# A hybrid decoder layer on one core: the FFN's planned order without lag between TensorE's steps, with leads by kind of step, and with the sums of weights and of activations in tiles of their own

## The chip, the cores and the metric

One Trainium2 chip, one of its cores. The metric is the time of one execution on the device in microseconds (us); lower is better.

## The reference, cut to what matters

The layer is a mixer (state-space and RWKV heads) followed by a gated FFN with a causal convolution. The change lies in the FFN:

```python
D_MODEL, SEQ, D_FF, FFN_CONV = 1024, 2048, 2816, 3
hn = _rms_norm(h, pre_ffn_norm)
u = _causal_dwconv(hn @ ffn_w_up, ffn_conv_w, ffn_conv_b)      # 2 * D_FF columns, 3 taps
gate, val = jnp.split(u, 2, axis=-1)
f = (jax.nn.silu(gate) * val) @ ffn_w_down
h = h + _rms_norm(f, post_ffn_norm)
```

Everything is float32. The kernel multiplies in float16: each operand is split into a high and a low half, and a product is three matmuls (high by high, high by low, low by high).

## The kernel before, in words

`phase_R` (RWKV) and `phase_S` (SSD, output projection, first norm) come first; then `phase_F`, the FFN. `phase_F` takes the tokens in two halves of 1024. For each of 22 blocks of hidden columns, counted by f, `Up.run` computes a gate and a value block with seven products in place of eight (a Strassen-like scheme in 2 by 2 blocks). Each product is 12 matmuls of 128x128 by 128x512 on line 1378, so an f has 84. Its weights are seven tiles `w0` to `w6`, one buffer each. In the first half they are made on the spot, in `Up.weights`: four blocks of `w_u` are loaded to a ring of six tiles `us`; POOL (GpSimd) forms sums of them, one into a small tile `ut` and the others in place in `us` (line 1350); ACT (ScalarE) writes the high half of `w` (line 1219) and DVE (VectorE) the low half (line 1226); SP (SyncE) stores each `w` in DRAM (line 1347). In the second half they are only loaded from there.

After the products of an f: ACT and DVE gather the PSUM banks into `C0` (one buffer) and `C1` (two buffers), on lines 1392 and 1396. ACT scales (line 1427), DVE adds two taps for the gate block `p` and two for the value block `a` (line 1431), ACT applies silu (line 1441), and DVE multiplies (line 1444). POOL copies the two carried columns in and out (`fcarry`, lines 1435 and 1437).

Two f make a pair. `Pair.factors` splits the pair's result into seven tiles `fa`: DVE sums in place (`p`, line 1484), POOL sums into a small tile `ft` (line 1484, two writes to the same tile), ACT writes the high halves (line 1219), POOL the low halves (line 1224). `down` then multiplies two pairs (at the end of a half, three) by the down weights: 168 matmuls on line 1614. Its weights `dw` are made from `r` (loads of 1 MB), with POOL sums in `r` and `rt` (line 1193), high halves on ACT (line 1575), low halves on DVE (line 1578), four tiles in a ring. DVE adds the banks to accumulators `acc` (line 1627). In the last down of the first half one pair has its weights in `dwx`, which borrows `C0`, `C1` and `a1`. `Half.tokens` loads and splits the activations into `b0` to `b6`, with a POOL sum in a small tile `ht`. `Finish.rows` does the last norm: squares into a scratch tile `fj` (line 1690), gains (line 1693), and the output rows `fin` (line 1706).

The small tiles `ht`, `ut`, `ft` and `fj` share one ring of two buffers with the tag `s3`. Each step that begins a use of it also "writes" the name `"s3"`, so that the uses follow each other in the order of the program text:

```python
op("G", 1.25, lambda: sub(x(), st[a11], st[a21]), (n[a11], n[a21]), (nt, "s3"))              # ut
(o, "s3") if o == nt and not t else (o,)                                                      # ft, both writes
```

What sets the order: `phase_F` doesn't emit its steps from f = 2 on, it hands them to a planner, `Program` (`op` is `Program.add`). A step has an engine (T for TensorE or PE, V for DVE, A for ACT, G for POOL, Q for SP's queue), an estimated duration, a function, and the names that it reads and writes. `Program.run` fixes TensorE's order as the text has it, gives each step a due time (counted back from the TensorE step that needs it), and then simulates the five engines: whenever one is free, the step with the earliest due time among the ready ones starts; an engine with a ready step never waits. A step's result is there after the step's duration and a lag of its engine, `LAG`. The simulated order is the order in which each engine's queue is written, and the engines then run their queues strictly in that order. In the text, the order is: steps of f, weights of f + 1, then every fourth f the down of two earlier pairs, then, at odd f, the factors of the pair. `last_down`, the down of the last pairs of the second half with the final norm, is emitted outside the planner, as is everything before f = 2.

Of the kernel before, what the change touches and what calls it, by code (L numbers as in the profile page):

```python
# [7 lines left out]
F32 = mybir.dt.float32  # L8
# [8 lines left out]
T = 2048  # L17
# [38 lines left out]
class Program:  # L56
# [2 lines left out]

    SHARED = 0.55, 0.75  # L60
    STORE = 4.0
    LAG = {"T": 0.25, "V": 0.12, "A": 0.14, "G": 0.12, "Q": 2.0}

    def __init__(self):
        self.on, self.ops, self.writer, self.readers, self.tensor, self.near, self.far = False, [], {}, {}, None, set(), set()

    def add(self, engine, us, fn, reads=(), writes=()):
        if not self.on:
            fn()
            return  # L70
        n = len(self.ops)
        before = set()
        for r in reads:
            if r in self.writer:
                before.add(self.writer[r])
            self.readers.setdefault(r, []).append(n)
        for w in writes:
            if w in self.writer:
                before.add(self.writer[w])
            before.update(self.readers.pop(w, ()))  # L80
            self.writer[w] = n
        if engine == "T":
            if self.tensor is not None:
                before.add(self.tensor)
            self.tensor = n
        if engine == "V" and any(r[0] in ("u", "d") for r in reads):
            self.near.add(n)
        if engine == "Q" and not writes:
            self.far.add(n)
        before.discard(n)  # L90
        self.ops.append((engine, us, fn, before))

    def run(self):
        ops = self.ops
        count = len(ops)
        after = [[] for _ in ops]
        for n, (_, _, _, before) in enumerate(ops):
            for b in before:
                after[b].append(n)
        due, at = [1e9] * count, 0.0  # L100
        for n, (engine, us, _, _) in enumerate(ops):
            if engine == "T":
                due[n] = at
                at += us
        for n in range(count - 1, -1, -1):
            engine, us, _, _ = ops[n]
            for a in after[n]:
                due[n] = min(due[n], due[a] - us - self.LAG[engine])
        left = [len(o[3]) for o in ops]
        ready = [0.0] * count  # L110
        wait = {k: [] for k in self.LAG}
        for n in range(count):
            if not left[n]:
                wait[ops[n][0]].append(n)

        now, order, busy, coming = 0.0, [], {}, []
        while len(order) < count or busy:
            for k, some in wait.items():
                if k in busy:
                    continue  # L120
                some = [n for n in some if ready[n] <= now + 1e-9]
                if some:
                    n = min(some, key=lambda n: (due[n], n))
                    wait[k].remove(n)
                    order.append(n)
                    busy[k] = [ops[n][1], n]
            rate = dict.fromkeys(busy, 1.0)
            if "V" in busy and "G" in busy and busy["V"][1] not in self.near:
                rate["V"], rate["G"] = self.SHARED
            step = min([v[0] / rate[k] for k, v in busy.items()] + [  # L130
                ready[n] - now for k, some in wait.items() if k not in busy for n in some])
            now += step
            for k in list(busy):
                busy[k][0] -= step * rate[k]
                if busy[k][0] < 1e-9:
                    n = busy.pop(k)[1]
                    for a in after[n]:
                        ready[a] = max(ready[a], now + self.LAG[k] + self.STORE * (a in self.far))
                        left[a] -= 1
                        if not left[a]:  # L140
                            wait[ops[a][0]].append(a)
        for n in order:
            ops[n][2]()
        self.__init__()
# [32 lines left out]
S_RIGHT = (  # L177
    "ident_s mhalf_s", "ssm pov por ss pnv pnr", "Y", "yr", "xi", "m", "gpost", "gpre2", "hT", "yt", "wo",
)
F_EARLY = ("us", "s3", "b0", "b1", "b2", "b3")  # L180
F_MID = (
    "p0", "p1", *(f"w{i}" for i in range(7)), "C0", "b4", "b5", "b6", "C1", "a1", "fpar mhalf_f fcarry",
)
# [979 lines left out]
def phase_F(tc, K, w_u, w_d, H, HN, out, halves=2):  # L1163
# [6 lines left out]
    with ExitStack() as ctx:  # L1170
# [25 lines left out]
            S.activation(hi, src, AF.Copy)  # L1196
            eng.tensor_tensor(out=lo, in0=src, in1=hi, op=ALU.subtract)

        def temp(name):
            return wk.tile([P, Q], F32, name=name, tag="s3", bufs=2)  # L1200

        prog = Program()
        op = prog.add
# [27 lines left out]
        class Half:  # L1231
# [10 lines left out]
            def part(self, k, wanted, nm):  # L1242
# [20 lines left out]

                        op("Q", 1., load, (), (name, "us" if ring else ("p", q)))
                n11, n21, n12, n22 = names
                nt = slot("s3", 2)

                def hold(*some):
                    return (*some, *(x[:2] for x in some if x[0] == "p"))
# [14 lines left out]

                def x():
                    if "t" not in h:
                        h["t"] = temp(f"ht{nm}{k}")
                    return h["t"]

                put(0, n11, lambda: h[0, 0])  # L1290
                minus(n12, n12, n11, lambda: (h[1, 0], h[1, 0], h[0, 0]))
                op("G", 1.25, lambda: sub(x(), h[1, 1], h[1, 0]), hold(n22, n12), (nt, "s3"))
                put(1, nt, x)
                put(2, n12, lambda: h[1, 0])
                if 3 in wanted:
# [8 lines left out]
        class Up:  # L1304
# [6 lines left out]
            def weights(self):  # L1311
# [11 lines left out]
                for s, c in ((1, 0), (0, 0), (1, 1), (0, 1)):  # L1323
# [6 lines left out]
                            pace(tc, K, d, 12)  # L1330

                    op("Q", .9, load, (), (n[s, c], "us"))
                nt = slot("s3", 2)

                def x():
                    if "t" not in st:
                        st["t"] = temp("ut" + nm).rearrange("p (a b) -> p a b", b=P)
                    return st["t"]

                def put(i, name, get):  # L1340
# [10 lines left out]

                a11, a12, a21, a22 = (0, 0), (0, 1), (1, 0), (1, 1)
                put(0, n[a11], lambda: st[a11])
                op("G", 1.25, lambda: sub(x(), st[a11], st[a21]), (n[a11], n[a21]), (nt, "s3"))
                plus(a21, a21, a22, ALU.add)
                plus(a11, a21, a11)
                put(1, n[a11], lambda: st[a11])
# [91 lines left out]
        class Pair:  # L1449
# [8 lines left out]
            def factors(self, u0, u1):  # L1458
                nm, a = self.nm, self.a
                tag = "w{}" if self.extra else f"fa{{}}{self.i % 2}"  # L1460
                nt, t = slot("s3", 2), []
                n11, n21, n12, n22 = ("p", 0, 0), ("p", 0, 1), ("p", 1, 0), ("p", 1, 1)
                src = {n11: (u0, 0), n21: (u0, Q), n12: (u1, 0), n22: (u1, Q)}

                def get(n):
                    if n == nt:
                        if not t:
                            t.append(temp("ft" + nm))
                        return t[0]
                    u, x = src[n]  # L1470
                    return u.p[:, x:x + Q]

                def put(i, n):
                    def parts():
                        if i not in a:
                            a[i] = wk.tile([P, 2, Q], F16, name=f"fa{i}{nm}", tag=tag.format(i))
                        return get(n), a[i][:, 0, :], a[i][:, 1, :]

                    hold = (n[:2],) if n != nt else ()
                    split_op((*self.fa[i], 0), (*self.fa[i], 1), parts, "V" if self.extra else "G", (n, *hold), ())  # L1480

                def plus(o, x, y, alu, e="G"):
                    hold = [n[:2] for n in (x, y) if n != nt]
                    op(e, {"G": 1.25, "V": .62}[e], lambda: {"G": G_, "V": V}[e].tensor_tensor(
                        out=get(o), in0=get(x), in1=get(y), op=alu), (x, y, *hold), (o, "s3") if o == nt and not t else (o,))

                put(0, n11)
                plus(nt, n11, n21, ALU.subtract)
                put(3, nt)
                plus(n21, n21, n22, ALU.add, "V")  # L1490
                plus(n11, n21, n11, ALU.subtract, "V")
                put(1, n11)
                plus(nt, n12, n11, ALU.subtract)
                put(4, n12)
                put(2, n21)
                put(5, nt)
                put(6, n22)
# [153 lines left out]
        class Finish:  # L1651
# [14 lines left out]
            def rows(self, q, t, eng, folded=False):  # L1666
# [10 lines left out]

                op("Q", 2., load, (), (nx,))
                for first, dh in zip((True, False), (1, 0) if q else (0, 1)):
                    nj = slot("s3", 2)  # L1680
                    nacc = ("acc", y[dh], t)

                    def c(dh=dh):
# [2 lines left out]
                    def square(c=c, dh=dh, first=first):  # L1686
                        if first:
                            x["ss"] = wk.tile([P, 2], F32, name=f"fss{tt}", tag="fss", bufs=2)
                        jk = wk.tile([P, 2 * Q], BF16, name=f"fj{tt}{dh}", tag="s3", bufs=2)
                        S.activation(jk[:, 0:Q], c(), AF.Square, scale=IWS, accum_out=x["ss"][:, dh:dh + 1])  # L1690

                    def gain(c=c, dh=dh):
# [1 line left out]

                    if (q or dh) and not folded:
                        op("G", 1.25, lambda c=c: add(c(), c(), acc[1][:, t]), (nacc, ("acc", 1, t)), (nacc,))
                    op("A", .75, square, (nacc,), (nj, "s3", (*ns, dh), *(((*ns, 1 - dh), (*ns, "r")) if first else ())))
                    op("V" if eng is V else "G", .62 if eng is V else 1.25, gain, (nacc, "gf"), (nacc,))

                def sums():  # L1700
# [205 lines left out]
```

## Time and profile before

| what | value |
|---|---|
| median of 3 runs | 2689.52 us (2687.17 to 2689.76) |
| profiled execution, its own time | 2683.97 us |
| its span, first to last instruction | 2681.7 us |
| mean granted TensorE clock | 0.971 |
| PE busy | 2475.0 us, 92% of the span |
| DVE, ACT, POOL busy | 1909.1, 1207.9, 1223.6 us |
| the planned part, about | 1437 to 2614 us after the span's start |

The span is shorter than the execution's time by what lies around the instructions, and the profiled execution is 5.55 us below the median of the runs. Matmuls are pipelined, so PE busy near 100% is not PE at its peak; how many matmuls a stretch holds says more. "A <-B" behind an idle time names the instruction that ended it. A group's mean duration mixes undisturbed and delayed instructions.

### The profile page before, as it was taken

The numbers are of one execution on the slowest core, as the hardware profiler recorded it, in microseconds if no ns is written. First come the engines' busy times: TensorE is split into PE (matmuls) and PEld (weight loads), VectorE is DVE, ScalarE is ACT, GpSimd is POOL, SyncE is SP. The second block draws the span as 40 slices with busy tenths as digits, with TensorE's granted clock in tenths as the row PEclk, the third lists the DMA queues.
The fourth block names the chain that finished last, engine by engine and source line by source line (L and its number), as shares of the span: only waits on it lengthen the run. The fifth ranks groups of instructions, "written<-read, shape, count | busy, mean of one in ns | idle before, by whom it ended". The sixth has DMA issues, their size and how long they took to land. (4 is left out here: it accounts for less than half of the span.)

```text
span 2681.7 us, 53948 instructions
## 1 busy us (share of the span) xinstructions
PE 2475.0 (92%) x21340; PEld 1556.0 (58%) x21340; DVE 1909.1 (71%) x3655; ACT 1207.9 (45%) x2467; POOL 1223.6 (46%) x1324
## 2 busy tenths in 40 slices
PE   5889999999999889999997899999999999999998
PEld 4788888888888855555543344444443444444443
DVE  6768777777777665567677868787789836465557
ACT  6445555555565453344444543434354333123132
POOL 2344444444545343234467565656657523222135
PEclk8899999999999989999999999999999999999999
DMA  6323232232223252334455434443435543333252
GB/s 212 73 61 73 53 60 57 65 81 53 57 60 73 89 174 98 107 115 143 128 194 171 156 138 157 134 169 122 159 124 188 183 149 100 103 102 102 87 158 106
DMA packets 309341, 310.74 MB, mean 116 GB/s; under 512 B 168160, under 2 KB 213600, under 8 KB 305760
## 3 DMA queue, kind: packets, MB, share of 16 engines
q1 hardware_dynamic: 307792, 305.72, 37.9%
q8 instruction: 167, 2.74, 0.4%
q10 hardware_dynamic: 1296, 1.58, 0.2%
q14 instruction: 86, 0.70, 0.1%
HBM read 187.85 MB, written 110.99 MB: 111 GB/s over the span
## 5 line engine op out<-in xcount | busy, mean ns | idle before, releaser
L1378 PE MATMUL u<-b,w 128*128 128x512 f16 x3696 | 816.6, 383 | 30.4 <-ACT w L1219 16.1
L1378 PEld LDWEIGHTS <-w 128*128 128x128 f16 x3696 | 363.3, 99 | 480.0 <-issue 29.7
L289 PE MATMUL d<-xt,wr 128*128 128x129 f16 x5376 | 336.9, 224 | 18.1 <-DMA xt<-xh 15.3
L1614 PE MATMUL d<-dw,fa 128*128 128x512 f16 x1512 | 336.4, 381 | 10.6 <-DVE dw L1578 8.4
L289 PEld LDWEIGHTS <-wr 128*128 128x128 f16 x5376 | 322.8, 100 | 32.5 <-ACT wr L252 15.2
L1614 PEld LDWEIGHTS <-fa 128*128 128x128 f16 x1596 | 157.2, 98 | 212.9 <-issue 26.9
L1396 DVE TENSOR_TENSOR C<-u,C 128x512 f32<-128x512 f32 x220 | 150.5, 685 | 163.0 <-PE u L1378 162.6
L289 PE MATMUL c<-xt,wc 128*128 128x131 f16 x3072 | 205.3, 227 | 23.3 <-ACT tr L429 10.4
L289 PEld LDWEIGHTS <-wc 128*128 128x128 f16 x3072 | 189.4, 100 | 39.9 <-issue 31.9
L1627 DVE TENSOR_TENSOR acc<-d,acc 128x512 f32<-128x512 f32 x212 | 140.2, 682 | 51.8 <-PE d L1614 51.2
L576 DVE TENSOR_TENSOR tmp<-atl,xl 128x60 f32<-128x60 f32 (+24 forms) x465 | 139.5, 300 | 44.9 <-DMA atl<-ATd 28.7
L1431 DVE SCALAR_TENSOR_TENSOR p<-C,fpar,p 128x1024 f32<-128x1024 f32 x88 | 126.4, 1437 | 57.0 <-ACT p L1427 53.6
L1224 POOL TENSOR_TENSOR fa<-p,fa 128x512 f16<-128x512 f32 x100 | 133.2, 1350 | 70.8 <-ACT fa L1219 70.8
L1226 DVE SCALAR_TENSOR_TENSOR w<-us,w 128x512 f16<-128x512 f32 x132 | 116.5, 889 | 61.2 <-ACT w L1219 60.2
L452 DVE SCALAR_TENSOR_TENSOR ca<-rc,cw,ca 128x128 f32<-128x128 f32 x384 | 132.3, 389 | 22.8 <-POOL ca L447 22.6
L1219 ACT ACTIVATE fa<-p 128x512 f16<-128x512 f32 x110 | 66.5, 626 | 162.6 <-DVE p L1444 138.8
L579 DVE TENSOR_TENSOR xl<-xl,tmp 128x60 f32<-128x60 f32 (+24 forms) x465 | 124.7, 268 | 11.3
L1437 POOL COPY fcarry<-C 128x2 f32<-128x2 f32 x88 | 36.1, 410 | 182.6 <-DVE C L1396 182.2
L1431 DVE SCALAR_TENSOR_TENSOR a<-C,fpar,a 128x1024 f32<-128x1024 f32 x88 | 114.3, 1299 | 6.4 <-ACT a L1427 4.6
L1219 ACT ACTIVATE w<-us 128x512 f16<-128x512 f32 x132 | 80.0, 622 | 81.0 <-POOL us L1350 61.9
L1392 ACT ACTIVATE C<-u 128x512 f32<-128x512 f32 x88 | 51.8, 589 | 142.7 <-PE u L1378 125.7
L689 POOL TENSOR_TENSOR tS<-S,Pi 64x256 f32<-64x256 f32 x64 | 40.4, 632 | 163.5 <-DVE S L699 161.1
(316 smaller groups left out, 4550.3 us busy)
## 6 DMA issues: line engine op xcount, KB each, us to landing
UW<-w SPq DMA_DIRECT2D x154, 256.0 KB
w<-UW SPq DMA_DIRECT2D x154, 256.0 KB
us<-in_w_u_dram SPq DMA_DIRECT2D x88, 256.0 KB
DW<-dw SPq DMA_DIRECT2D x70, 256.0 KB
dw<-DW SPq DMA_DIRECT2D x56, 256.0 KB
hs<-HN SPq DMA_DIRECT2D x48, 256.0 KB
r<-in_w_d_dram SPq DMA_DIRECT2D x10, 1024.0 KB
xin<-in_x_dram SPq DMA_DIRECT2D x16, 512.0 KB
```

The source lines that it names most:

```text
L289: nc.tensor.matmul(ps, w[:, a, kt, :], xt[:, b, kt, cols], start=n == 0, stop=n == 3 * KT - 1)
L452: V.scalar_tensor_tensor(out=acc[:, q], in0=raw[:, q, k:k + 128], scalar=cw[:, g + q, k:k + 1], in1=acc[:, q], op0=ALU.mult, op1=ALU.add)
L576: chain.tensor_tensor(out=tmp[:, :m, :n], in0=atl[:, j, j + 1:32].unsqueeze(1).to_broadcast([P, m, n]), in1=xl[:, :m, j:j + 1].to_broadcas ...
L579: chain.tensor_tensor(out=xl[:, :m, j + 1:32], in0=xl[:, :m, j + 1:32], in1=tmp[:, :m, :n], op=ALU.add)
L1219: S.activation(h, src, AF.Copy, **({} if scale is None else {"scale": scale}))
L1224: {"V": V, "G": G_}[engine].tensor_tensor(out=l, in0=src, in1=h, op=ALU.subtract)
L1226: V.scalar_tensor_tensor(out=l, in0=src, scalar=scale, in1=h, op0=ALU.mult, op1=ALU.subtract)
L1378: nc.tensor.matmul(bk[at], self.w[i][:, u, k, :], self.half.b[i][:, k, v, :], start=start and n == 0, stop=n == 11, skip_group_check=True)
L1396: op("V", .61, lambda: V.tensor_tensor(out=part(j, x), in0=bk[at], in1=part(*a), op=ALU.add), (("u", 4 * s + at), (*(c0, c1)[a[0]], a[1])) ...
L1431: V.scalar_tensor_tensor(out=o[j], in0=C[j][:, 2 - d:1026 - d], scalar=cw[:, g, 2 - d:3 - d], in1=o[j], op0=ALU.mult, op1=ALU.add)
L1614: nc.tensor.matmul(bk[s, t], pairs[m].a[i][:, u, t * P:t * P + P], pairs[m].w[n][0][:, v, :], start=new and m == 0 and u == v == 0, stop=m ...
L1627: V.tensor_tensor(out=acc[j][:, t], in0=bk[s, t], in1=acc[j][:, t], op=ALU.add)
```

## The change

Four things, all in the planner's input or in the tiles; no arithmetic changes and no instruction is added or removed.

- Between two TensorE steps the planner no longer counts `LAG["T"]` (0.25), neither in the due times nor in the simulation.
- Each step gets a kind: its engine, the least of the names that it writes, the least of those it reads ("-" for none). `LEAD` maps 21 kinds to a number of microseconds. The choice among ready steps is by due time less lead.
- The ring `s3` of two becomes two tiles of one buffer each, `s3` and `s4`, with the same bytes in all: `ut` in `s3`, `ft` in `s4`, `ht` in `s4` for the first half and in `s3` for the second, the scratch `fj` in one or the other by its half of the columns.
- The name `"s3"` is no longer written, so uses of one tile follow each other only through that tile.

```diff
+    LEAD = {"A C0 u": 21, "A p p": 20, "A w us": 23, "G cy C1": 36, "G fa fa": 6, "G rt r": -38, "Q r -": -4, "Q us -": -40, "V C0 C0": 27, "V C1 C0": 9, "V C1 C1": 1, "V a1 C1": 7, "V acc acc": -4, "V b b": 3, "V dw dw": 2, "V hx acc": 11, "V p C0": 8, "V p a1": -2, "V p p": 7, "V w p": 16, "V w us": -4}
...
+        self.kinds.append(" ".join([engine, *(min([x[0] for x in some if isinstance(x, tuple)] or ["-"]) for some in (writes, reads))]))
...
             for a in after[n]:
-                due[n] = min(due[n], due[a] - us - self.LAG[engine])
+                if engine != "T" or ops[a][0] != "T":
+                    due[n] = min(due[n], due[a] - us - self.LAG[engine])
...
-                    n = min(some, key=lambda n: (due[n], n))
+                    n = min(some, key=lambda n: (due[n] - self.LEAD.get(self.kinds[n], 0.0), n))
...
-                        ready[a] = max(ready[a], now + self.LAG[k] + self.STORE * (a in self.far))
+                        lag = self.STORE * (a in self.far) + self.LAG[k] * (k != "T" or ops[a][0] != "T")
+                        ready[a] = max(ready[a], now + lag)
...
-F_EARLY = ("us", "s3", "b0", "b1", "b2", "b3")
+F_EARLY = ("us", "s3", "s4", "b0", "b1", "b2", "b3")
...
-        def temp(name):
-            return wk.tile([P, Q], F32, name=name, tag="s3", bufs=2)
+        def temp(name, tag):
+            return wk.tile([P, Q], F32, name=name, tag=tag)
...
-                op("G", 1.25, lambda: sub(x(), st[a11], st[a21]), (n[a11], n[a21]), (nt, "s3"))
+                op("G", 1.25, lambda: sub(x(), st[a11], st[a21]), (n[a11], n[a21]), (nt,))
...
-                nt, t = slot("s3", 2), []
+                nt, t = ("s4", 0), []
...
-                        out=get(o), in0=get(x), in1=get(y), op=alu), (x, y, *hold), (o, "s3") if o == nt and not t else (o,))
+                        out=get(o), in0=get(x), in1=get(y), op=alu), (x, y, *hold), (o,))
```

Kinds that the text below names: "A w us" and "V w us" are the high and low halves of the up weights, "Q us -" the loads of `us`, "A C0 u" and "V C1 C0" gathers of an up bank, "V p C0" and "V a1 C1" the taps, "A p p" silu, "V acc acc" the gathers of a down bank and the final gains, "V dw dw" and "V C0 C0" the low halves of `dw` and `dwx`, "G fa fa" the low halves of `fa`, "G rt r" sums into `rt`, "V hx acc" the output rows.

More of the change, by code (lines that the diff above doesn't have):

```diff
@@ L65, in __init__ @@
         self.on, self.ops, self.writer, self.readers, self.tensor, self.near, self.far = False, [], {}, {}, None, set(), set()
+        self.kinds = []
     def add(self, engine, us, fn, reads=(), writes=()):
@@ L1265, in part @@
                 n11, n21, n12, n22 = names
-                nt = slot("s3", 2)
+                nt = (f"s{4 - hf}", 0)
                 def hold(*some):
@@ L1286, in x @@
                     if "t" not in h:
-                        h["t"] = temp(f"ht{nm}{k}")
+                        h["t"] = temp(f"ht{nm}{k}", f"s{4 - hf}")
                     return h["t"]
@@ L1291, in part @@
                 minus(n12, n12, n11, lambda: (h[1, 0], h[1, 0], h[0, 0]))
-                op("G", 1.25, lambda: sub(x(), h[1, 1], h[1, 0]), hold(n22, n12), (nt, "s3"))
+                op("G", 1.25, lambda: sub(x(), h[1, 1], h[1, 0]), hold(n22, n12), (nt,))
                 put(1, nt, x)
@@ L1332, in weights @@
                     op("Q", .9, load, (), (n[s, c], "us"))
-                nt = slot("s3", 2)
+                nt = ("s3", 0)
                 def x():
                     if "t" not in st:
-                        st["t"] = temp("ut" + nm).rearrange("p (a b) -> p a b", b=P)
+                        st["t"] = temp("ut" + nm, "s3").rearrange("p (a b) -> p a b", b=P)
                     return st["t"]
@@ L1467, in get @@
                         if not t:
-                            t.append(temp("ft" + nm))
+                            t.append(temp("ft" + nm, "s4"))
                         return t[0]
@@ L1679, in rows @@
                 for first, dh in zip((True, False), (1, 0) if q else (0, 1)):
-                    nj = slot("s3", 2)
+                    nj = (f"s{3 + dh}", 0)
                     nacc = ("acc", y[dh], t)
@@ L1688, in square @@
                             x["ss"] = wk.tile([P, 2], F32, name=f"fss{tt}", tag="fss", bufs=2)
-                        jk = wk.tile([P, 2 * Q], BF16, name=f"fj{tt}{dh}", tag="s3", bufs=2)
+                        jk = wk.tile([P, 2 * Q], BF16, name=f"fj{tt}{dh}", tag=f"s{3 + dh}")
                         S.activation(jk[:, 0:Q], c(), AF.Square, scale=IWS, accum_out=x["ss"][:, dh:dh + 1])
@@ L1696, in rows @@
                         op("G", 1.25, lambda c=c: add(c(), c(), acc[1][:, t]), (nacc, ("acc", 1, t)), (nacc,))
-                    op("A", .75, square, (nacc,), (nj, "s3", (*ns, dh), *(((*ns, 1 - dh), (*ns, "r")) if first else ())))
+                    op("A", .75, square, (nacc,), (nj, (*ns, dh), *(((*ns, 1 - dh), (*ns, "r")) if first else ())))
                     op("V" if eng is V else "G", .62 if eng is V else 1.25, gain, (nacc, "gf"), (nacc,))
```

## The prediction

> **What bounds the kernel now.** I read, in this order, the page's totals and slices, the chain of waits, the table of three stretches, PE's waits, and then the order of each engine around one stall. A row of the chain gives PE's own pace:
>
> ```profile
> span 2681.7 us, 53948 instructions
> 2197.64 72.52 PE u L1378 x336
> ```
>
> 336 matmuls in 72.52 us without a stop are 0.2158 us each. Three stretches of the planned part (columns: window, its length, then busy time and count of PE, PE's loads, DVE, ACT and POOL, granted clock, DMA share, GB/s):
>
> ```profile
> 1437.00:2000.00 563.00, 527.29 (x2359) 232.07 (x2358) 445.61 (x515) 254.09 (x390) 340.02 (x285) 0.97 0.43 147
> 2000.00:2082.00 82.00, 70.62 (x311) 30.80 (x309) 81.60 (x90) 33.58 (x64) 57.42 (x43) 0.96 0.53 177
> 2082.00:2614.00 532.00, 532.00 (x2458) 240.79 (x2457) 298.40 (x351) 157.74 (x214) 161.05 (x195) 1.00 0.40 121
> ```
>
> The second half (from 2082) is solid PE: 2458 matmuls at 0.2158 are 530 of 532 us, with DVE at 56%. Nothing can be won there. The three rows hold 5128 matmuls, 1107 us of work in 1177 us: 70 us are lost, nearly all before 2082. They are the most that a better order can bring. PE's waits there name their causes (us, times, longest):
>
> ```profile
> PE u L1378 <- ACT w L1219: 16.1, 6, 3.6
> PE u L1378 <- DVE C L1396: 9.2, 6, 4.8
> PE d L1614 <- DVE dw L1578: 8.4, 14, 2.0
> PE d L1614 <- DVE dwx L1578: 4.3, 3, 2.9
> PE u L1378 <- ACT C L1392: 3.9, 1, 3.9
> PE d L1614 <- ACT dw L1575: 2.1, 2, 1.9
> PE d L1614 <- ACT dwx L1575: 1.8, 1, 1.8
> PE u L1378 <- DVE w L1226: 0.9, 3, 0.5
> ```
>
> Together 46.7 us. The other 23 us come behind the stalls, as slower matmuls:
>
> ```profile
> 1706.82 35.55 PE L1378 MATMUL u<-b,w 128*128 128x512 f16 x156 [2.50 <-ACT w L1219]
> 1707.00:1710.50 3.50, 3.42 (x10) 0.57 0.60 176
> 1710.50:1740.00 29.50, 29.50 (x138) 1.00 0.51 167
> ```
>
> After a wait of 2.50 us the granted clock is 0.57 for about 3.5 us, with 10 matmuls where 16 fit; 156 matmuls take 35.55 us in place of 33.7. So I price each us of PE's waits at 70 / 46.7 = 1.5 us. The Trainium skill (TensorE: Matmul & The Clock Gate, Part 1: The HAM clock gate) states that the clock halves after an idle window of about 3.4 us and returns after as long a busy one. The half clock and its length agree; a wait of 2.50 us sufficed, and the trace decides. By that figure taken as a threshold, waits of 2.50 us would cost only themselves, and the forecast below would be 2661, two thirds of the gain.
>
> **Part 1: sums of weights no longer follow sums of activations.** This is the stall before 1706.82, on POOL:
>
> ```profile
> 1686.77 1.69 POOL L1435 COPY C<-fcarry 128x2 f32<-128x2 f32 x2 [4.78 <-ACT a L1427]
> 1692.20 4.29 POOL L1224 TENSOR_TENSOR fa<-p,fa 128x512 f16<-128x512 f32 x3 [3.75 <-ACT fa L1219]
> 1696.46 1.26 POOL L1484 TENSOR_TENSOR ft<-p,p 128x512 f32<-128x512 f32 x1
> 1697.68 1.15 POOL L1224 TENSOR_TENSOR fa<-p,fa 128x512 f16<-128x512 f32 x1
> 1698.80 1.26 POOL L1193 TENSOR_TENSOR ut<-us,us 128x512 f32<-128x512 f32 x1
> 1700.02 1.60 POOL L1224 TENSOR_TENSOR fa<-ft,fa 128x512 f16<-128x512 f32 x1
> 1701.58 1.72 POOL L1350 TENSOR_TENSOR us<-us,us 128x512 f32<-128x512 f32 x1
> ...
> 1704.38 1.72 POOL L1350 TENSOR_TENSOR us<-us,us 128x512 f32<-128x512 f32 x1
> ...
> 1677.35 0.67 DVE L1226 SCALAR_TENSOR_TENSOR w<-ut,w 128x512 f16<-128x512 f32 x1
> ```
>
> PE waits for the second weight of f = 11 (after a down come f = 9 and 10 with 7 products each and product 0 of f = 11). That weight needs two sums in `us` (1701.58, 1704.38), these overwrite what `ut` reads, so `ut` (1698.80) comes first; and `ut` had to follow the second write of `ft` (1696.46) by the name "s3" alone. `ft` in turn waits for the convolution, the gate and the DVE sums of the pair before. With its own tile `ut` waits only for the former `ut`'s low half, which ended at 1678.0, and POOL stands idle for 4.78 and 3.75 us ahead of 1692. The three sums take 1.26 + 1.72 + 1.72 = 4.7 us, so they fit there some 10 us earlier, against a wait of 2.50. The same place comes at each odd f that has no down ahead of it, which is the row of six waits: 16.1 + 0.9 = 17.0 us, times 1.5 is 25.5. I take nine tenths, 23: what is late next is `fa`, moved back by 4.7 us, and it isn't read before the next down. What it could cost: one buffer in place of two makes `ut` wait for the former low half on DVE; bounds are nothing and one more wait of this size (2.5 times 1.5) at each of 20 f, 75 us. I take nothing, since the row at 1677.35 is 20 us ahead of the need. `ft`, `ht` and `fj` keep uses that POOL's or ACT's queue already separates: nothing. Ahead of the planned part `ut` of f = 2 starts at most 2 us later, with 35 us to its product.
>
> **Part 2: no lag between PE's steps.** The real PE has none (0.2158 times 12 is 2.59, the planner's 2.6). The old plan put PE at 2.85 a product and 1.55 in place of 1.3 in a down, so it believed that other engines had 10 to 16% more time than they have, and sorted work that frees a bank or feeds the next product behind work that could wait. Two places show that:
>
> ```profile
> 1757.41 0.67 DVE L1226 SCALAR_TENSOR_TENSOR w<-us,w 128x512 f16<-128x512 f32 x1
> 1758.01 0.68 DVE L1578 SCALAR_TENSOR_TENSOR dw<-r,dw 128x512 f16<-128x512 f32 x1
> 1758.74 0.81 PE L1614 MATMUL d<-dw,fa 128*128 128x512 f16 x3 [0.41 <-DVE dw L1578]
> ...
> 2079.43 1.75 DVE L1706 SCALAR_TENSOR_TENSOR fin<-acc,for,fin 128x512 f32<-128x512 f32 x1
> 2081.10 0.68 DVE L1396 TENSOR_TENSOR C<-u,C 128x512 f32<-128x512 f32 x1
> ...
> 2081.84 79.55 PE L1378 MATMUL u<-b,w 128*128 128x512 f16 x360 [4.78 <-DVE C L1396]
> ```
>
> A `dw` half stands one `w` half too late, and 4.78 us are lost because output rows of the first half, which must be done only before the next down (after the 79.55 us of this row), stand ahead of the bank that PE needs. With true due times and the leads (`dw` +2, `w` and `acc` -4) I expect the waits for `dw`, 10.5 us or 16 with the factor, to halve: 8. The waits for `C`, 13.1 us or 20, to halve too: 10. The lead of 11 for output rows works against this, 9 or 1 for the gathers, which is why I don't take all. Waits for `dwx`, 6.1 us or 9, get a lead of 27, but DVE there is busy for 81.60 of 82 us, so what one step gains another loses: 2. Bounds for each: nothing and the whole.
>
> **Part 3: the other leads.** High halves of the up weights (+23), silu (+20), carries (+36) move ahead on ACT and POOL, loads of `us` (-40) back on SP. Since an engine with a ready step never waits in the plan, a lead only decides between steps ready together; ACT and POOL are busy for 254 and 340 of 563 us, so this has room. Cost taken: nothing. SP's queue does block:
>
> ```profile
> 1687.63 13.32 SPq L1347 DMA_DIRECT2D UW<-w  x3
> ```
>
> A load behind such a block comes 13 us late, but the six-tile ring holds the two blocks that `ut` reads a whole f (18 us) ahead. From below a lead could bring no more than the rest of the 70.
>
> **The sum.** 23 + 8 + 10 + 2 = 43 us. The profiled execution took 2683.97, so 2641 for such a one; the median of the runs lay 5.55 above it, so I forecast 2646.5 for the median.
>
> **The rivals.** *Nearly all goes*: the second half shows that a plan with room keeps PE solid for 532 us. Then 65 of the 70 go: 2624. For it: POOL and ACT have room. Against: DVE would be busy for 445.61 of 509 us (2359 matmuls at 0.2158), 88%.
>
> *DVE becomes the bound*: up to 2000 DVE idles 117 us over 20 f (2 to 21), 5.9 us per f; my forecast leaves 563 - 39 - 446 = 78, 3.9 per f. If DVE can't get below 5 in queues that run strictly in order, the first half gains 18 and the seam at 2082 about 4: 2667. For it: the planner doesn't know slow instructions like the 1.75 us of the row at 2079.43, beside 0.74 elsewhere. The Trainium skill (SBUF — State Buffer, Who interferes with whom) states that a VectorE instruction with two SBUF inputs and a GpSimd one that reads SBUF exclude each other; moving POOL's sums into its idle time puts them beside other DVE steps, and the sum by that rule is this rival's.
>
> *Slower*: steps that wait for PE now stand earlier in ACT's and DVE's queues, because the planned PE is faster than one that stalls and drops its clock. A high half of `w` at the head of ACT's queue waits for PE's product to free its tile, and the scale and silu behind it come late, and with them DVE's taps. It decides when DVE's idle time rises over the present 5.9 us per f; each us more is 20 us. At 8 us: 2689.5 + 42 - 10 (the seam) = 2721. Against it: the rows of before show PE's results waiting for DVE, not the other way, except in gathers.
>
> *It doesn't do what it says*: new waits replace the old ones; 2689.5.
>
> **How the numbers follow.** Forecast 0.50, its own range 2632 to 2660; nearly all 0.20; DVE-bound 0.15; no change 0.05; slower 0.10. About 0.2% (5 us) is what a measurement of this kernel can tell from no change. Faster: 0.50 + 0.20 + 0.13 = 0.83; same 0.07; slower 0.10. The range runs from 2618, below the full gain, to 2680, above the DVE-bound case; it leaves out the slower case and most of no change.
>
> **What would show it.** Part 1: no `ut` behind `ft` at odd f, and the wait for ACT `w` near 2 us from 16.1. Part 2: no wait of 4.78 near 2075, waits for `dw` near 5. The first half's planned part from 1437 ends near 2040 in place of 2082, and the rest keeps its 600 us. Wrong if new waits for `w` come at even f (single `ut`), if SP's loads show as POOL's wait, or if the second half gets holes.

## The result, and the profile after

The changed kernel takes 2652.61 us (median of 4 runs, 2649.05 to 2657.98) beside 2688.35 us of the kernel before (4 runs, 2685.15 to 2689.76). The ratio is 0.9868 (95% interval 0.9852 to 0.9883): faster by 1.3%. The forecast for the median was 2646.5, with a range of 2618 to 2680. Lines of the kernel move down by 5.

The page's first line, PE's waits in the planned part, and three stretches (to the last down of the first half, then to the second half's solid part, then that) answer to those of before:

```profile
span 2653.5 us, 53912 instructions
```
```profile
PE u L1383 <- DVE C L1401: 7.1, 6, 2.4
PE d L1619 <- DVE dwx L1583: 6.0, 3, 3.5
PE u L1383 <- ACT C L1397: 5.7, 2, 4.9
PE u L1383 <- ACT w L1224: 5.1, 1, 5.1
PE d L1619 <- DMA dw<-DW: 2.5, 2, 1.4
PE d L1619 <- DVE dw L1583: 2.3, 4, 0.9
PE d L1619 <- ACT dwx L1580: 1.7, 1, 1.7
```
```profile
1437.00:1974.00 537.00, 518.54 (x2368) 231.96 (x2367) 484.87 (x514) 256.96 (x392) 375.73 (x287) 0.99 0.46 155
1974.00:2055.00 81.00, 71.99 (x324) 31.90 (x323) 80.33 (x90) 33.62 (x62) 53.01 (x39) 0.98 0.53 176
2055.00:2587.00 532.00, 528.92 (x2450) 239.11 (x2449) 304.60 (x355) 157.50 (x216) 166.16 (x198) 1.00 0.40 122
```

The first 514 DVE instructions of the planned part now end at 1974, where it took to 2000 before, and the second half begins its solid part at 2055, where it was 2082. Behind that nothing moved (532 us in both). PE's waits fell from 46.7 to 30.4 us. The wait for ACT `w` happens once and not six times, and that for `dw` fell from 10.5 to 2.3. The waits for `C` (DVE and ACT rows) are 12.8 where they were 13.1. And DVE is busy for 485 us where it was 446, with as many instructions: this is what the forecast had not seen.

The sums of f = 11, the example of the prediction, on POOL:

```profile
1668.85 1.64 POOL L1198 TENSOR_TENSOR ut<-us,us 128x512 f32<-128x512 f32 x1
...
1674.48 1.27 POOL L1355 TENSOR_TENSOR us<-us,us 128x512 f32<-128x512 f32 x1
...
1684.60 1.57 POOL L1355 TENSOR_TENSOR us<-us,us 128x512 f32<-128x512 f32 x1 [4.86 <-ACT fa L1224]
1691.42 1.72 POOL L1489 TENSOR_TENSOR ft<-p,p 128x512 f32<-128x512 f32 x1
```

`ut` stands 23 us ahead of the `ft` write that it had to follow, and the last of the two sums in `us` ends at 1686, before PE asks for it at 1693. There is no stall for `w` here any more.

### The profile page after: what moved, and what is told of

Read it like the earlier page. It is cut to its first block, busy times and chain, and to the rows that moved or that the text cites. A ratio compares the mean times of both kernels' runs of the same rounds, so it can differ in the third digit from the quotient of the medians.

```text
span 2653.5 us, 53912 instructions
## 1 busy us (share of the span) xinstructions
PE 2454.5 (93%) x21324; PEld 1551.8 (58%) x21340; DVE 1951.9 (74%) x3655; ACT 1210.2 (46%) x2467; POOL 1258.0 (47%) x1324
## 3 DMA queue, kind: packets, MB, share of 16 engines
q10 hardware_dynamic: 1296, 1.58, 0.2%
## 5 line engine op out<-in xcount | busy, mean ns | idle before, releaser
L294 PE MATMUL c<-xt,wc 128*128 128x131 f16 x3072 | 204.0, 227 | 21.7 <-ACT tv L434 10.6
L294 PEld LDWEIGHTS <-wc 128*128 128x128 f16 x3072 | 188.2, 100 | 36.0 <-issue 29.5
L1229 POOL TENSOR_TENSOR fa<-p,fa 128x512 f16<-128x512 f32 x100 | 142.7, 1441 | 41.5 <-ACT fa L1224 41.5
L1231 DVE SCALAR_TENSOR_TENSOR w<-us,w 128x512 f16<-128x512 f32 x132 | 143.1, 1094 | 24.7 <-ACT w L1224 23.1
L1436 DVE SCALAR_TENSOR_TENSOR a<-C,fpar,a 128x1024 f32<-128x1024 f32 x88 | 125.6, 1427 | 4.1 <-ACT a L1432 2.3
L1355 POOL TENSOR_TENSOR us<-us,us 128x512 f32<-128x512 f32 x66 | 105.5, 1602 | 48.6 <-DVE w L1231 31.0
```

What stands on the lines that cost most here:

```text
L294: nc.tensor.matmul(ps, w[:, a, kt, :], xt[:, b, kt, cols], start=n == 0, stop=n == 3 * KT - 1)
L1229: {"V": V, "G": G_}[engine].tensor_tensor(out=l, in0=src, in1=h, op=ALU.subtract)
L1231: V.scalar_tensor_tensor(out=l, in0=src, scalar=scale, in1=h, op0=ALU.mult, op1=ALU.subtract)
L1436: V.scalar_tensor_tensor(out=o[j], in0=C[j][:, 2 - d:1026 - d], scalar=cw[:, g, 2 - d:3 - d], in1=o[j], op0=ALU.mult, op1=ALU.add)
```

## The experiments

The kernels were timed in three groups, each beside the kernel before on one chip, where its median was 2680.5, 2684.4 and 2682.2 us; ratios are what to compare. Where the text sets a figure of one group beside one of another, it does so by the ratios.

**The split tiles alone** (lag kept, `LEAD = {}`).

> The split of the small tiles alone: ut in s3, ft in s4, no common name, with the lag between PE's steps kept and no leads. Theory (the terms of the prediction are separate): PE's wait for ACT w falls from 16.1 us to about 2, and 23 us go, 2665 by the median of before (2688). Rival (the plan works only as a whole: with a PE that it believes slow the freed sums are put anywhere): under 8 us, 2680 or more, and the wait for w stays over 8 us.

Ratio 1.0015 (1.0000 to 1.0029), 2684.0 us: the theory's mechanism is right and its time is wrong. PE's waits:

```profile
PE u L1382 <- DVE C L1400: 19.4, 10, 5.4
PE d L1618 <- DVE dw L1582: 12.5, 14, 1.9
PE u L1382 <- ACT C L1396: 10.1, 5, 4.4
PE u L1382 <- ACT w L1223: 2.5, 1, 2.5
PE u L1382 <- DVE w L1230: 0.4, 1, 0.4
```

17.0 us of waits for `w` became 2.9, as predicted. The waits for `C` took their place: 29.5 from 13.1. So the order by the name "s3" did cause the stalls (the one of f = 3 alone stays), but behind each of the others stood another wait about as long: 2.3 to 2.6 us on a gather of DVE at f = 7, 11, 15 and 19, and 4.4 us on one of ACT at f = 21. At f = 11 it came about like this:

```profile
1714.71 2.18 POOL L1354 TENSOR_TENSOR us<-us,us 128x512 f32<-128x512 f32 x1 [0.70 <-DVE w L1230]
1716.92 0.63 ACT L1223 ACTIVATE w<-us 128x512 f16<-128x512 f32 x1 [1.88 <-POOL us L1354]
1717.58 0.69 DVE L1230 SCALAR_TENSOR_TENSOR w<-us,w 128x512 f16<-128x512 f32 x1 [1.22 <-ACT w L1223]
1718.19 0.68 DVE L1400 TENSOR_TENSOR C<-u,C 128x512 f32<-128x512 f32 x1
...
1718.92 23.47 PE L1382 MATMUL u<-b,w 128*128 128x512 f16 x108 [2.55 <-DVE C L1400]
```

The gather stands in DVE's queue behind a low half; the low half waits for ACT's high half, and that for a sum on POOL, which takes 2.18 us where the two sums in the prediction's rows took 1.72 each.

**No lag alone** (old ring and name, `LEAD = {}`), and **the leads alone** (old ring, lag kept).

> No lag between PE's steps alone, old ring of two small tiles with its common name, no leads. Theory: the six waits for ACT w stay (16 us), waits for dw and C shrink by a third to a half; 8 to 15 us go, 2673 to 2680. Rival (an order for a faster PE puts steps that wait for PE at the head of in-order queues): slower than before, over 2693.

> The 21 leads alone, with the lag kept and the old ring. Theory: waits for w stay at 16 us since the common name still orders ut behind ft; waits for C shrink somewhat; 5 to 10 us go, 2678 to 2683. Rival (leads only fit the order that they were set for): slower than before, over 2693.

Ratios 0.9983 (0.9968 to 0.9997) and 0.9982 (0.9968 to 0.9996): under 5 us each by the ratio, at the lower end of the theory's size for the leads and below it for the lag. The lag alone:

```profile
PE u L1383 <- ACT w L1224: 18.3, 6, 5.1
PE u L1383 <- DVE w L1231: 13.0, 5, 3.2
PE u L1383 <- DVE C L1401: 6.6, 4, 2.4
PE d L1619 <- DVE dw L1583: 0.3, 1, 0.3
```

It does to `C` what the prediction said (13.1 to 6.6) and more than that to `dw` (10.5 to 0.3), and the waits for `w` take back most of it: 17.0 to 31.3. The leads alone bring `w` to 14.0 (6.8 on ACT and 7.2 on DVE), leave `C` at 12.3 and raise `dw` to 15.0.

**The changed kernel with the order of the small tiles kept.**

```diff
-                op("G", 1.25, lambda: sub(x(), st[a11], st[a21]), (n[a11], n[a21]), (nt,))
+                op("G", 1.25, lambda: sub(x(), st[a11], st[a21]), (n[a11], n[a21]), (nt, "sx"))
...
-                        out=get(o), in0=get(x), in1=get(y), op=alu), (x, y, *hold), (o,))
+                        out=get(o), in0=get(x), in1=get(y), op=alu), (x, y, *hold), (o, "sx") if o == nt else (o,))
```

(and likewise for `ht`.)

> The changed kernel, but every use of ht, ut and ft writes a common name again, so that these uses follow each other in the order of the text, though each has its own tile. Theory (it is the name that made the stalls, not the number of buffers): the waits for ACT w at odd f come back, about 16 us, and the time is 2653 + 20 to 25 = 2673 to 2678. Rival (the gain came from lag and leads, which find another way round the name): within 5 us of the changed kernel, 2648 to 2658.

Ratio 0.9968 (0.9955 to 0.9981), 2672.1 us. The waits for `w` are back, with two tiles or not; those for `C` and `dw` are almost gone:

```profile
PE u L1383 <- ACT w L1224: 18.3, 6, 5.2
PE u L1383 <- DVE w L1231: 9.8, 5, 3.2
PE u L1383 <- DVE C L1401: 3.0, 2, 2.4
PE d L1619 <- DVE dw L1583: 1.1, 2, 0.9
```

The theory holds: the common name is the cause of the stalls, and tiles of their own do nothing against it while the name stands. With the lag and the leads in place, doing away with the name is worth 10 of 1000 (0.9968 to 0.9871 in the run below), some 26 us; done first, it was worth nothing.

**The changed kernel again, without leads, and with the lag.**

> The changed kernel once more, beside the partial ones on one chip. Both theories: ratio 0.985 to 0.990 to before.

> Split tiles and no lag, without leads. Theory (split tiles and a true pace of PE need each other: the one frees the sums, the other orders DVE's gathers ahead of them): most of the gain, 2655 to 2665 where before is 2680. Rival (the leads carry it): over 2672.

> Split tiles and leads, with the lag kept. Theory: gathers get their leads of 9 and 1 but due times of a slow PE, so about half of the gain, 2660 to 2672 where before is 2680, with PE's waits for C and dw between those of the split tiles alone (29.5 and 12.5 us) and of the changed kernel (12.8 and 2.3). Rival (the lag does nothing beside the leads): as the changed kernel, within 4 us of it.

Ratios 0.9871 (0.9852 to 0.9889), 0.9900 (0.9876 to 0.9924) and 0.9957 (0.9943 to 0.9972). So with the split tiles the lag is worth about 9 of 1000, the leads about 3, and the intervals of the first two overlap. Without leads most of the gain is there, as the theory had it, and the waits for `C` are 17.1 us. With the lag kept a third of the gain is left, where the theory said half; the waits for `C`, 19.7 us, lie between those of the split tiles alone and of the changed kernel, as expected, but those for `dw`, 13.5, lie above both:

```profile
PE u L1382 <- ACT C L1396: 13.6, 7, 5.6
PE d L1618 <- ACT dw L1579: 8.7, 4, 2.5
PE u L1382 <- DVE C L1400: 6.1, 5, 3.7
PE d L1618 <- DVE dw L1582: 4.8, 8, 1.9
```

The parts by themselves come to +1.5, -1.7 and -1.8 of 1000, together to -13. They don't add: as the waits above show, each part alone takes away one kind of wait, and another kind grows in its place.

**Why DVE is late.** For the same work, from f = 2 to the down with `dwx`, the windows of before, of the split tiles alone, and of the changed kernel are (the same columns as in the table of stretches):

```profile
1437.00:1999.25 562.25, 526.54 (x2356) 231.68 (x2354) 445.17 (x514) 253.81 (x390) 340.02 (x285) 0.97 0.43 147
```
```profile
1437.00:1999.60 562.60, 522.57 (x2368) 232.47 (x2366) 492.62 (x516) 254.10 (x392) 366.21 (x287) 0.99 0.43 148
```
```profile
1439.00:1973.80 534.80, 516.34 (x2358) 230.96 (x2357) 483.29 (x512) 255.45 (x391) 374.95 (x285) 0.99 0.46 155
```

DVE's busy time rises from 445 to 493 us with 514 and 516 instructions of the same kinds. By groups, first before and then the split tiles alone:

```profile
L1226 DVE SCALAR_TENSOR_TENSOR w<-us,w 128x512 f16<-128x512 f32 x115 | 99.3, 870 | 51.5 <-ACT w L1219 50.8
L1396 DVE TENSOR_TENSOR C<-u,C 128x512 f32<-128x512 f32 x100 | 68.0, 682 | 13.4 <-PE u L1378 13.2
```
```profile
L1230 DVE SCALAR_TENSOR_TENSOR w<-us,w 128x512 f16<-128x512 f32 x116 | 128.6, 1111 | 26.9 <-ACT w L1223 26.1
L1400 DVE TENSOR_TENSOR C<-u,C 128x512 f32<-128x512 f32 x101 | 68.2, 680 | 4.2 <-PE u L1382 4.1
```

The low halves of `w`, which read two tiles in SBUF, went from 870 to 1111 ns; the gathers of `C`, which read a bank and one tile, stayed at 682 and 680. The Trainium skill (SBUF — State Buffer, Who interferes with whom) states just this: a VectorE instruction with two SBUF inputs and a GpSimd one that reads SBUF shut each other out, and one with at most one SBUF input, outside certain faster modes, is left alone. The trace agrees. Sorted one by one by whether a TENSOR_TENSOR of POOL ran at any time beside them, the low halves of `w` with none beside them take 681 ns before and 682 ns with the split tiles, those with one 1069 and 1392 ns, and the gathers of `C` 679 to 682 ns either way. What changed is how often and how long they run together: 56 of 115 low halves had one beside them before, 70 of 116 have with the split tiles, and the time that they share rose from 49 to 83 us. POOL's instructions lengthen too (`ut` from 1418 to 1827 ns). To see whether this costs time, **POOL's share was cut in the same order**:

```diff
-                if scale is None:
-                    {"V": V, "G": G_}[engine].tensor_tensor(out=l, in0=src, in1=h, op=ALU.subtract)
+                if scale is None and engine == "G":
+                    G_.tensor_tensor(out=l[:, 0:64], in0=src[:, 0:64], in1=h[:, 0:64], op=ALU.subtract)
+                    G_.memset(l[:, 64:Q], 0.0)
+                elif scale is None:
+                    V.tensor_tensor(out=l, in0=src, in1=h, op=ALU.subtract)
```

> Split tiles alone, in the same order, but POOL computes only 64 of the 512 columns of each low half of fa in the first and second half's pairs and sets the others to zero (that part of fa is left out). Theory (POOL's sums, let loose, run beside DVE's instructions and stretch them: DVE busy from 1437 to 2000 rose from 446 to 493 us at the same 516 instructions): with some 100 us of POOL's reads gone, DVE is busy under 460 us there, PE's wait for C falls from 29.5 to under 15 us, and the time is under 2668. Rival (the waits for C come from the order alone, DVE's stretch is only idle time filled): waits for C stay over 22 us and the time over 2675.

Ratio 0.9843 (0.9824 to 0.9862), 2642.0 us, from 1.0015 for the same order with whole instructions. Waits for `C` fall to 10.8 us. The same work:

```profile
1437.00:1955.25 518.25, 510.73 (x2351) 229.94 (x2350) 448.69 (x512) 251.78 (x390) 311.25 (x348) 1.00 0.47 159
```
```profile
L1233 DVE SCALAR_TENSOR_TENSOR w<-us,w 128x512 f16<-128x512 f32 x115 | 105.1, 916 | 27.2 <-ACT w L1223 26.8
```

(The window to 2000, which the expectation named, still holds 493 us of DVE, but for 565 instructions.) DVE's idle time is the same in both, 562.6 - 492.6 = 70.0 and 518.3 - 448.7 = 69.6 us; the stretch is shorter by 44 us, and so is DVE's busy time (4 us of it is work that the second window lacks, 2351 matmuls and not 2368). The low halves with no TENSOR_TENSOR beside them again took 681 ns. The theory holds: the gain of the split tiles was paid back as longer DVE instructions. A shorter POOL queue also delivers its sums sooner, as the rows of f = 11 above would ask, and this run can't part the two. Nor did every kind shorten: the taps of `p` took 1705 and 1706 ns in the two.

**The same cut in the changed kernel.**

> The changed kernel with the short low halves of fa of the run before (64 of 512 columns computed, the others zero; that part is left out). Theory (what is left of PE's waits before 2055 is also DVE held up by POOL): 2625 to 2640, waits for C under 6 us. Rival (the rest is order and start, not contention): within 6 us of the changed kernel, 2644 to 2656.

Ratio 0.9809 (0.9788 to 0.9831), 2632.6 us; waits for `C` 7.4 us, a little over what was expected, and the wait of 5.1 us for `w` is gone. About 17 us of what was left (0.9871 to 0.9809) went with POOL's low halves of `fa`.

**The carried columns on ACT** (`S.activation(..., AF.Copy)` in place of `G_.tensor_copy`, with an estimate of 0.2).

> The changed kernel with the copies of the two carried columns on ACT in place of POOL (L1440 and L1442: 0.68 and 0.67 us each there, 54 us before 2055, most of it waiting). Theory (fewer reads on POOL, less hold-up): 3 to 8 us faster than the changed kernel, 2643 to 2648. Rival (ACT's queue, strictly in order, waits for the gathers at these copies and holds up scales and high halves): slower than the changed kernel by 5 us or more.

Ratio 0.9908 (0.9887 to 0.9929), 2657.4 us: the rival, by its size; the waits for `dw` rise to 10.4 us and those for `w` to 10.6. DVE has no relief (481.53 us for 510 instructions). Its low halves of `w` took 1196 ns on the mean, where the changed kernel's took 1096. Whether the copies held DVE up on POOL, or only waited there, this run doesn't show.

**Low halves of `fa` on DVE**, three of seven, then all (`"V" if self.extra or i in (0, 4, 6) else "G"`, and all of 0 to 6).

> The changed kernel with three of the seven low halves of a pair's fa (0, 4, 6) on DVE in place of POOL, 0.68 against 1.58 us. Theory (POOL's time is what stretches DVE: some 30 instructions of 1.58 us less on POOL by 1974, 20 us more on DVE undisturbed): 3 to 10 us faster than the changed kernel, 2640 to 2648. Rival (DVE is the bound and any work added to it is paid): 10 us or more slower, over 2660.

> The same with all seven low halves on DVE: 68 instructions by 1974, 46 us more on DVE undisturbed, 109 us less on POOL. Theory: still not slower than the changed kernel, 2640 to 2652. Rival (DVE is the bound): 20 us or more slower, over 2670.

Ratios 0.9853 (0.9831 to 0.9875) and 0.9820 (0.9796 to 0.9843), 2643.8 and 2633.4 us. Neither is slower, against the rival. The first is faster than the changed kernel by the theory's size, but the intervals overlap (0.9852 to 0.9889 for the changed kernel); the second is clear of it, and faster than its theory's range. With all of them on DVE:

```profile
1437.00:1955.48 518.48, 509.42 (x2340) 229.22 (x2339) 492.00 (x573) 251.18 (x387) 280.11 (x216) 0.99 0.46 157
```
```profile
L1231 DVE SCALAR_TENSOR_TENSOR w<-us,w 128x512 f16<-128x512 f32 x114 | 102.8, 912 | 6.0 <-ACT w L1224 5.5
L1229 DVE TENSOR_TENSOR fa<-p,fa 128x512 f16<-128x512 f32 x50 | 46.6, 939 | 1.1 <-ACT fa L1224 0.7
```
```profile
2021.29 90.81 PE L1383 MATMUL u<-b,w 128*128 128x512 f16 x420
```

Some 60 more instructions stand on DVE, and its busy time is 492 us where the changed kernel's was 483 (573 and 512 instructions), since the others are shorter. The window holds 18 matmuls fewer than that of the changed kernel, 4 us of work, and is 16 us shorter. The last row is the seam into the second half: 420 matmuls without a stop. This is the fastest of the kernels that compute all of the layer, 5 of 1000 below the changed one (0.9820 beside 0.9871, each against the kernel before on its own chip).

## Why the prediction was right or wrong

**Right**: what bounds the kernel, the place and the cause of the stalls at odd f, and the seam near 2082, where 4.78 us became 1.32 and 0.60, in PE's order of the changed kernel:

```profile
2052.41 2.75 PE L1383 MATMUL u<-b,w 128*128 128x512 f16 x12 [1.32 <-DVE C L1401]
2055.76 75.27 PE L1383 MATMUL u<-b,w 128*128 128x512 f16 x348 [0.60 <-DVE C L1401]
```

The price of 1.5 us for each us of PE's wait was near: PE lost 41 us to 30.4 us of waits between 1435 and 2587 (1152 us for 5149 matmuls at 0.2158), 1.3 for one. The gain is 35.7 us between the medians, of the 43 forecast. The two profiled executions lie 28.7 us apart (2683.97 and 2655.30), and this is what the traces account for: PE's loss went from 70 to 41 us. The first half's planned part ends at 2055, 27 us earlier, where the forecast said 2040.

**Wrong, by terms.** Part 1, 23 us: the waits for `w` went from 17.0 to 5.1 us, 2 expected; the one left is that of f = 3, at the start. The value was wrong: alone the part brought nothing. The step that failed is "what is late next is `fa`, moved back by 4.7 us, and it isn't read before the next down"; late next were the gathers of `C`, most of them on DVE (13.1 us of waits before, 29.5 with the split tiles alone). Part 2, `dw`, 8 us: too small, waits went from 10.5 to 2.3 and not to 5. Part 2, `C`, 10 us: nothing, 13.1 to 12.8; the order was mended (6.6 with no lag alone, 3.0 and 0.5 with the name kept), and it was lost again when POOL's sums were free, most likely to DVE's longer instructions: with POOL's low halves cut short in the changed kernel it is 7.4. `dwx`, 2 us: it got worse, 6.1 to 7.7. New are 2.5 us in the second half for `dw` from DRAM, behind loads on SP's queue. A slip that changed no term: 2.85 for 2.6 and 1.55 for 1.3 are 10 to 19% more time, not 10 to 16%.

That the sum came out near is in part luck: it added terms that don't add. Split tiles, lag and leads give +1.5, -1.7 and -1.8 of 1000 alone. Part 1 is near its 23 us only when it comes last (26), and then the other two bring 3 of 1000, some 9 us, where the forecast had 20.

**What could have been read.** The prediction says that "the planner doesn't know slow instructions" and holds DVE's busy time at 446 us. But the planner has them: with `SHARED = 0.55, 0.75` it lets a step of DVE go at 0.55 and one of POOL at 0.75 of its speed while both run, save for DVE's steps that read a bank. The 1.75 us of the prediction's row at 2079.43 stand beside sums of `acc` on POOL (from 2077.71 to 2080.64); the two of 0.74 before it (2075.70 and 2076.97) don't. So that filling POOL's idle time costs DVE's time stood in the kernel's text, as a model.

**The rivals.** *DVE becomes the bound* (2667, given 0.15) was farther off in time than the forecast but names what took the gain back, with its reason. It had the wrong form: DVE's idle time fell to 51 us over 20 f, 2.6 per f, below the forecast's 3.9, since the busy time which I held fixed at 446 us rose to 483. *Slower* and *no change* didn't happen. *Nearly all goes* (2624, a ratio of 0.976) wasn't reached by any run; the nearest are those that take POOL's low halves off it, 0.9809 and 0.9820.

## What to carry to other kernels

Before pricing the removal of a wait, ask what is late next and try the parts alone: here each part by itself was worth under 0.2%, and the three together 1.3%. An engine's busy time is not a constant of the work: where two engines hold each other up, as DVE and POOL do here, filling one's idle time lengthens the other's instructions, so look at the mean duration of a group of each kind, not only at the share. Then try the work on the other engine, even if that is the busier one.

## What the runs showed of the hardware that was not expected

The size of the hold-up: DVE's low halves with two SBUF inputs took 870, 1111 and 912 ns on the mean as POOL's busy time over the same work was 340, 366 and 280 us, while gathers from a bank took 680 to 682 throughout. Moving the low halves of `fa` from POOL (1.58 and 1.67 us each in the changed kernel) to DVE made DVE's busy time only 9 us longer, though 69 of them take 61 us there (46.6 and 14.9 us); its window lacks six other instructions, some 7 us.
